# First two tiles of the up product as eight plain block products, with the operand sums of the other units issued behind them

## The chip, the cores and the metric

One NeuronCore of one Trainium2 chip. The time is device microseconds (us) of one launch, which runs a whole encoder layer for two request groups together: 1024 prompt frames and 64 sample frames, 1088 columns in all. The kernel before takes 1810.93 us (median of three executions, 1809.39 to 1812.55).

## The reference, cut to what matters

All arithmetic is float32. The mixers and the memory attention come first, and the change lies where the memory attention ends and the MLP begins:

```
x = x + mix @ w_out
x = x + mem_attend(rmsnorm(x) * norm_mem) @ w_mo
h = rmsnorm(x) * norm_ffn                    # per frame 1/sqrt(mean(x*x) + eps)
x = x + square(relu(h @ w_up)) @ w_down      # w_up 1024 x 4096, w_down 4096 x 1024
y = rmsnorm(x) * norm_final
```

## The kernel before, in words

**Layout.** Activations are held transposed: feature blocks of 128 rows (`KD` = 8 blocks for 1024 features) by frames. The frames are cut into two groups, `GR`: group 0 has 512 columns, group 1 has 576. A float32 product is made of three passes: each operand is cut by `split` (L169 to L171) into a high part (ACT copies it to a rounded type) and a low part (DVE subtracts the high part from the source), and TensorE multiplies high by high, high by low and low by high. So every operand costs one ACT pass and one DVE pass, and every block product three matmuls for each 128-row block.

**The product ahead of the change.** `dense_add(1, w_mo, ...)` adds the memory attention's output to the residual of group 1, in two halves of the contraction. The second half (HALF, `store=True`) goes through the eight output blocks in the order 0, 4, 1, 5, 2, 6, 3, 7. For each block m it loads a 512-column weight tile, splits it, runs 24 matmuls (two column chunks, 320 and 256), adds both chunks to `xT[1][m]` on DVE (L1083), stores the block to HBM (L1085), and then calls `after(m)`, which is `forms`.

**The up product.** h @ w_up is computed in 16 units (`NU`), each giving two 128-row tiles of the hidden layer for both groups. A unit is a 2 x 2 block product (the two halves of the contraction, the two output tiles, the two groups) and is done with seven block products in place of eight: one each with B11, B21, T1, T2, B22, T3 and T4. B11 and B21 are group 0's normalised blocks (`h3`, ready long before). B22 is group 1's blocks 4 to 7. T1 to T4 are sums and differences of blocks of both groups. On the weight side `sums` (four DVE passes) and five `split`s make S1 to S4 and A22 for every unit. Products with group 1 have two column halves of 288, in two PSUM banks (`mul2`); products of group 0 have 512 columns in one bank (`mul`). The `i < 2` branch is another grouping of the same seven products. The squared hidden tiles go to HBM (`hid_d`), to be read again by the down product.

**What `forms` does.** For every m: the square of x (ACT) and its running sum (DVE, L1038), which later becomes the mean square of group 1. From m = 4 on, with k = m - 4: the two blocks k and k + 4 of group 1 are normalised (L1059, with the norm of the layer before, `rm1`), four differences are made (L1270 to L1278) and five operands split (T1, B22, T2, T3, T4). The missing factor between the two norms, `q`, is made from the running sum by a matmul with ones (`pr`) and `rstd_chain` (L149 to L154), and multiplies the unit's results of group 1 in `square`.

**The order of work.** Each engine runs its instructions in the order that a planner wrote. The planner goes through them in its own simulated time, and where several are ready for one engine it takes the one with the lowest `tc.cur_priority`, a number that counts up by one with every instruction issued in the program. The lines that set it here: `dense_add` adds 600 around `after(m)` and takes it off again, and `tc.cur_priority += 1200` (L1284) stands between the dense product and the loop over units. DMAs are issued by SP, in its own queue.

**Buffers.** Raw weights `wr` and split weights `wh`, `wl` have two buffers each. Operands sit in units of 576 columns: `ap` (16), `xt` (16), `aq` (12), `tm` (4), and `fz` (12). The PSUM pool of the loop, `psm`, has two banks `pw` (tag w) and three pairs `pz` (tag z).

Of the kernel before, what the change touches and what calls it, by code (L numbers as in the profile page):

```python
# [9 lines left out]
F32R = mybir.dt.float32r  # L10
# [3 lines left out]
ALU = mybir.AluOpType  # L14
# [3 lines left out]
P = 128  # L18
D = 1024
KD = D // P  # L20
# [32 lines left out]
def kernel(ctx: ExitStack, tc: tile.TileContext, *args):  # L53
    nc = tc.nc
# [10 lines left out]
    w_up, w_down = w_up[0], w_down[0]  # L65
# [103 lines left out]
    def split(hi, lo, src):  # L169
        act(hi, src, AF.Copy)  # L170
        V.tensor_tensor(out=lo, in0=src, in1=hi.bitcast(F32), op=ALU.subtract)  # L171
# [10 lines left out]
    def load_w(src, r0, kt, c0, dst=None):  # L182
        raw = early.pop(c0) if src is w_in and c0 in early else fetch_w(src, r0, kt, c0)
        hi, lo = dst or (wp.tile([P, KD, P], F32R, name=nm, tag=nm) for nm in ("wh", "wl"))
        split(hi[:, :kt], lo[:, :kt], raw)
        return hi, lo
# [35 lines left out]
    def pair(which):  # L222
        return [pools[which].tile([P, 576], F32R, name="ap", tag="ap") for _ in range(2)]
# [18 lines left out]
    with ExitStack() as pa:  # L242
# [5 lines left out]
        xt = []  # L248
# [217 lines left out]
    def halves(t):  # L466
        return t[:, :PAST], t[:, PAST:]
# [551 lines left out]
    def unit(tag, dt=F32):  # L1019
        return units[tag].tile([P, 576], dt, name=tag, tag=tag)  # L1020
# [20 lines left out]
    def rms_stats(g, psum, tag, tiles=None, keep=False, s2=None):  # L1041

        if not s2:
            for k in range(KD):
                s2 = add_square(g, k, s2, wide())
        rr = unit("tm")
        for c0, cn in GR[g][2]:
            ps = psum.tile([P, 512], F32, name="pr", tag=tag)
            mm(ps[:, :cn], ones, s2[:, c0:c0 + cn], True, True)
            v, t = tiles or (unit("tm"), unit("tm"))  # L1050
            rstd_chain(None, cn, ps[:, :cn], "xxx", scale=1.0 / D, out=rr[:, c0:c0 + cn], tiles=(v, t))
            if keep:
                V.tensor_tensor(out=t[:, :cn], in0=v[:, :cn], in1=rr[:, c0:c0 + cn], op=ALU.mult)
                nc.sync.dma_start(out=rms_d[:, c0:c0 + cn], in_=t[:, :cn])
        return rr

    def normed(g, k, gains, rr, c0, cn, out=None):
        hf = unit("tm") if out is None else out
        V.scalar_tensor_tensor(out=hf[:, :cn], in0=xT[g][k][:, c0:c0 + cn], scalar=gains[:, k:k + 1],  # L1059
                               in1=rr[:, c0:c0 + cn], op0=ALU.mult, op1=ALU.mult)  # L1060
        return hf
# [10 lines left out]
    def dense_add(g, src, r0, kt, a, psum, ahead=None, store=False, after=None, order=None):  # L1072

        t0, n, _ = GR[g]
        for m in (0, 4, 1, 5, 2, 6, 3, 7) if after else range(KD):
            w = load_w(src, r0, kt, m * P)
            if ahead:
                ahead(m)
            for c0, cn in GR[g][2]:
                ps = psum.tile([P, 512], F32, name="pa", tag="mm")  # L1080
                mm3(ps[:, :cn], w, lambda k: (a[k][0][:, c0:c0 + cn], a[k][1][:, c0:c0 + cn]), kt, order=order)
                xs = xT[g][m][:, c0:c0 + cn]
                V.tensor_tensor(out=xs, in0=xs, in1=ps[:, :cn], op=ALU.add)  # L1083
            if store:
                nc.sync.dma_start(out=x2_d[m][:, t0:t0 + n], in_=xT[g][m])  # L1085
            if after:
                tc.cur_priority += 600
                after(m)
                tc.cur_priority -= 600
# [135 lines left out]
    def bank():  # L1225
        return psm.tile([P, 512], F32, name="pw", tag="w", bufs=2)

    def banks():
        return psm.tile([P, 2, 512], F32, name="pz", tag="z", bufs=3)
# [4 lines left out]
    def mul(ps, w, b, start, cols):  # L1234

        for k, (bh, bl) in enumerate(b):
            last = k == len(b) - 1
            mm(ps, w[0][:, k], bh[:, cols], start and k == 0, False, skip_group_check=not start)
            mm(ps, w[0][:, k], bl[:, cols], False, False, skip_group_check=not start)
            mm(ps, w[1][:, k], bh[:, cols], False, last, skip_group_check=not start)  # L1240
# [9 lines left out]
    hb = {B11: h3[:4], B21: h3[4:]}  # L1250
    for f in (T2, T1, B22):
        hb[f] = [[late.pop(0)() for _ in range(2)] for k in range(4)]
    for f in (T3, T4):
        hb[f] = [[unit("xt" if k else "ap", F32R) for _ in range(2)] for k in range(4)]

    sums2 = []

    def forms(m):

        if m == 0:  # L1260
            sums2.append(add_square(1, 0, None, unit("tm")))
        else:
            add_square(1, m, sums2[0], unit("tm"))
        if m < 4:
            return
        k = m - 4
        (h11, h12), (h21, h22) = ((xw[0][i], xw[1][i]) for i in (k, k + 4))
        for i in (k, k + 4):
            normed(1, i, g_ffn, rm1, 0, N2, xw[1][i])
        V.tensor_tensor(out=h11[:, :N1], in0=h12[:, :N1], in1=h11[:, :N1], op=ALU.subtract)  # L1270
        act(h11[:, N1:], h12[:, N1:], AF.Copy)
        split(*hb[T1][k], h11)
        V.tensor_tensor(out=h12, in0=h22, in1=h12, op=ALU.subtract)
        split(*hb[B22][k], h22)
        V.tensor_tensor(out=h22, in0=h22, in1=h11, op=ALU.subtract)
        split(*hb[T2][k], h22)
        split(*hb[T3][k], h12)
        V.tensor_tensor(out=h21[:, :N1], in0=h21[:, :N1], in1=h22[:, :N1], op=ALU.subtract)  # L1278
        split(hb[T4][k][0][:, :N1], hb[T4][k][1][:, :N1], h21[:, :N1])

    dense_add(1, w_mo, HALF * P, KD - HALF, om[HALF:], ps1, store=True, after=forms)
    pm1.close()
    psm = ctx.enter_context(tc.tile_pool(name="psm", bufs=2, space=PSUM))
    tc.cur_priority += 1200  # L1284
    for t in t1s:
        Q.memset(t[:, N1:], 0.0)

# [20 lines left out]
    def plus(out, a, b, eng=V):  # L1308
        eng.tensor_tensor(out=out, in0=a, in1=b, op=ALU.add)  # L1309

    for i in range(NU):
        r1 = fetch_w(w_up, 0, KD, 2 * i * P)
        r2 = fetch_w(w_up, 0, KD, (2 * i + 1) * P)
        pa, pb = ([wp.tile([P, KD, P], F32R, name=nm, tag=nm) for nm in ("wh", "wl")] for _ in range(2))
        split(*pa, r1)
        s1 = fz.tile([P, 4, P], F32, name="s1", tag="s1", bufs=1)
        sums(r1[:, :4], r1[:, 4:], r2[:, :4], r2[:, 4:], s1, V)
        S2, S1 = wform(r1[:, :4]), wform(s1)
        S3 = wform(r2[:, :4])
        S4, A22 = [t[:, :4] for t in pb], [t[:, 4:] for t in pb]  # L1320
        split(*S4, r1[:, 4:])
        split(*A22, r2[:, 4:])
        t1 = t1s[i % 2]
        W, Z, X = bank(), banks(), banks()
        mul(W, [t[:, :4] for t in pa], hb[B11], True, slice(0, N1))
        act(t1[:, :N1], W, AF.Copy)
        c12, c22 = unit("ap"), unit("ap")
        if i < 2:

            mul(W, [t[:, 4:] for t in pa], hb[B21], False, slice(0, N1))  # L1330
            Y = banks()
            mul2(Y, S4, hb[B22], True)
            plus(halves(c12), halves(t1), Y[:, :, :HN])
        mul2(Z, S2, hb[T2], True)
        plus(halves(c12), halves(c12 if i < 2 else t1), Z[:, :, :HN])
        mul2(X, S1, hb[T1], True)
        plus(halves(c22), halves(t1), X[:, :, :HN])
        if i < 2:
            plus(halves(c12), halves(c12), X[:, :, :HN])
        else:  # L1340
            mul(W, [t[:, 4:] for t in pa], hb[B21], False, slice(0, N1))
        c11 = unit("xt")
        square(c11[:, :N1], W)
        if i == 0:
            q = rms_stats(1, psm, "w", s2=sums2[0])
            rms = unit("tm")
            nc.sync.dma_start(out=rms, in_=rms_d)
            V.tensor_tensor(out=q, in0=q, in1=rms, op=ALU.mult)
        mul2(Z, S3, hb[T3], False)
        plus(halves(c22), halves(c22), Z[:, :, :HN])  # L1350
        square(c22, c22, q)
        if i >= 2:
            mul2(X, S4, hb[B22], False)
            plus(halves(c12), halves(c12), X[:, :, :HN])
        square(c12, c12, q)
        mul2(Z, A22, hb[T4], False, N1)
        c21 = unit("xt")
        plus(c21[:, :HN], t1[:, :HN], Z[:, 0, :HN])
        plus(c21[:, HN:N1], t1[:, HN:N1], Z[:, 1, :N1 - HN])
        square(c21[:, :N1], c21[:, :N1])  # L1360
        for m, g, t in ((0, 0, c11), (0, 1, c12), (1, 0, c21), (1, 1, c22)):
            t0, n, _ = GR[g]
            nc.sync.dma_start(out=hid_d[2 * i + m][:, t0:t0 + n], in_=t[:, :n])
    fz_ctx.close()


# [122 lines left out]
```

## Time and profile before

| what | value |
|---|---|
| median of three executions | 1810.93 us (1809.39 to 1812.55) |
| the profiled execution: time | 1812.65 us |
| the profiled execution: span, first to last instruction | 1810.6 us |
| mean granted TensorE clock | 0.982 of full |
| PE busy | 1731.0 us, 96% |
| PE weight loads busy | 1516.8 us, 84% |
| DVE busy | 1199.6 us, 66% |
| ACT busy | 794.2 us, 44% |

The span is the profiled execution; its time has 2.05 us more around it. PE is the row of matmuls, DVE the vector engine, ACT the scalar engine. The second half of the dense product ends at 1049.7 us of the span, and the loop over units runs from there to about 1420 us.

### The profile page before, as it was taken

How to read it: one execution, taken by the hardware profiler on the slowest of the kernel's cores; microseconds unless marked ns; L12 is line 12 of the kernel's file. 1: busy time of each engine (PE TensorE's matmuls, PEld its weight loads, DVE VectorE, ACT ScalarE, POOL GpSimd, SP SyncE). 2: the span in 40 equal slices, each digit the busy share in tenths (PEclk: the TensorE clock that was granted, in tenths of full speed). 3: DMA queues.
4: the chain of work that ended last, by engine and by line, in shares of the span. 5: the costliest groups of instructions: out<-in, count | busy, mean ns of one | idle time of the engine just before them, and what ended most of it. 6: DMA issues, size and time to landing. Idle time of an engine off the chain costs nothing.

```text
span 1810.6 us, 29643 instructions
## 1 busy us (share of the span) xinstructions
PE 1731.0 (96%) x11454; PEld 1516.8 (84%) x11467; DVE 1199.6 (66%) x2362; ACT 794.2 (44%) x1619; POOL 96.9 (5%) x201
## 2 busy tenths in 40 slices
PE   7999999999999998899999959999999999999997
PEld 5877757778877877898899949999999999999987
DVE  6455778979887887856777696555555544444435
ACT  6464566455537843535556443434334312222113
POOL 3011202000220200000000000000000000000000
PEclk9999999999999999999999979999999999999999
DMA  7221212231223456422432322333334833222112
GB/s 243 83 77 37 64 46 75 69 82 60 84 89 98 139 159 214 119 85 63 142 104 72 95 85 95 98 104 104 116 105 133 317 97 97 96 90 66 47 35 100
DMA packets 227596, 184.87 MB, mean 102 GB/s; under 512 B 16510, under 2 KB 196415, under 8 KB 227455
## 3 DMA queue, kind: packets, MB, share of 16 engines
q1 hardware_dynamic: 227199, 182.96, 32.5%
q8 instruction: 90, 1.47, 0.4%
q14 instruction: 51, 0.42, 0.1%
q0 software_dynamic: 256, 0.01, 0.1%
HBM read 132.45 MB, written 50.44 MB: 101 GB/s over the span
## 4 chain that ended last, share of the span: by engine, by line
PE 56%; DVE 4%; ACT 1%; DMA 1%; issue 1%; DVEq 0%; ACTq 0%
PE pz L71 24%; PE pw L71 16%; PE pa L71 8%; PE pq L71 5%; PE pmo L71 1%; PE pms L71 1%; DVE y L767 0%; PE pmt L1144 0%; DVE ap L171 0%; PE pz L1414 0%; DVE wl L171 0%; ACT wh L74 0%; DVE tm L1059 0%; DVE xt L1083 0%; DVE xt L1059 0%
## 5 line engine op out<-in xcount | busy, mean ns | idle before, releaser
L74 ACT ACTIVATE wh<-wr 128x1024 fp32r<-128x1024 f32 (+1 forms) x180 | 161.4, 905 | 426.4 <-PE pz L71 195.4
L171 DVE TENSOR_TENSOR wl<-wr,wh 128x1024 fp32r<-128x1024 f32 (+1 forms) x180 | 184.8, 1034 | 67.9 <-ACT wh L74 66.9
L71 PE MATMUL pw<-ap,wh 128*128 128x512 f32 x704 | 220.0, 394 | 1.3 <-ACT t L74 0.7
L71 PE MATMUL pa<-ap,wh 128*128 128x512 f32 (+2 forms) x768 | 192.1, 337 | 5.4 <-DVE xt L1083 3.3
L71 PE MATMUL pz<-ap,wh 128*128 128x288 f32 x960 | 192.5, 294 | 0.0
L71 PE MATMUL pm<-hx,wh 128*128 128x512 f32 (+1 forms) x640 | 178.4, 366 | 2.0 <-ACT wh L74 2.0
L71 PE MATMUL pm<-ap,wh 128*128 128x256 f32 (+1 forms) x768 | 164.9, 308 | 0.0
L71 PEld LDWEIGHTS pz<-ap,wh 128*128 128x128 f32 x960 | 156.7, 188 | 4.9 <-DVE ap L1309 0.4
L71 PEld LDWEIGHTS pa<-ap,wh 128*128 128x128 f32 x768 | 134.6, 194 | 17.7 <-DVE xt L1083 3.4
L71 PEld LDWEIGHTS pw<-ap,wh 128*128 128x128 f32 x704 | 127.8, 189 | 23.8 <-ACT t L74 1.2
L71 PE MATMUL pw<-ap,wl 128*128 128x512 f32 x352 | 138.2, 392 | 5.6 <-DVE wl L171 5.6
L71 PE MATMUL pz<-ap,wl 128*128 128x288 f32 x480 | 141.0, 294 | 0.0
L71 PE MATMUL pa<-ap,wl 128*128 128x512 f32 (+2 forms) x384 | 128.8, 337 | 2.8 <-DVE wl L171 2.8
L71 PEld LDWEIGHTS pm<-hx,wh 128*128 128x128 f32 x640 | 111.3, 192 | 21.8 <-ACT wh L74 2.6
L71 PEld LDWEIGHTS pm<-ap,wh 128*128 128x128 f32 x768 | 124.1, 192 | 5.2 <-issue 1.9
L767 DVE SCALAR_TENSOR_TENSOR y<-ext,cwT,y 128x288 f32<-128x288 f32 (+2 forms) x300 | 125.3, 443 | 3.1
L1309 DVE TENSOR_TENSOR xt<-xt,pz 128x576 f32<-128x576 f32 x56 | 42.2, 753 | 114.4 <-PE pz L71 107.9
L71 PE MATMUL pm<-ap,wl 128*128 128x256 f32 (+1 forms) x384 | 114.3, 298 | 0.0
L71 PE MATMUL pm<-hx,wl 128*128 128x512 f32 (+1 forms) x320 | 112.8, 353 | 0.2 <-DVE wl L171 0.2
L1309 DVE TENSOR_TENSOR xt<-xt,pw 128x512 f32<-128x512 f32 (+2 forms) x80 | 51.0, 638 | 70.0 <-PE pw L71 67.7
L71 PE MATMUL pq<-ap,wh 128*128 128x512 f32 (+2 forms) x384 | 93.1, 331 | 0.0
L74 ACT ACTIVATE sba<-sba 128x127 f32<-128x127 f32 (+8 forms) x102 | 68.1, 682 | 55.2 <-DVE sba L490 54.4
(371 smaller groups left out, 3647.4 us busy)
## 6 DMA issues: line engine op xcount, KB each, us to landing
wr<-in_w_up_dram SPq DMA_DIRECT2D x32, 512.0 KB
wr<-in_w_down_dram SPq DMA_DIRECT2D x32, 512.0 KB
wr<-in_w_in_dram SPq DMA_DIRECT2D x24, 512.0 KB
hid_d<-ap SPq DMA_DIRECT2D x32, 288.0 KB
aq<-hid_d SPq DMA_DIRECT2D x32, 288.0 KB
wr<-in_w_out_dram SPq DMA_DIRECT2D x16, 512.0 KB
wr<-in_w_mq_dram SPq DMA_DIRECT2D x16, 512.0 KB
wr<-in_w_mo_dram SPq DMA_DIRECT2D x32, 256.0 KB
```

Source lines behind the costliest of these rows:

```text
L71: nc.tensor.matmul(out, lhsT=lhsT, rhs=rhs, start=start, stop=stop, **kw)
L74: nc.scalar.activation(out=out, in_=in_, func=func, **kw)
L171: V.tensor_tensor(out=lo, in0=src, in1=hi.bitcast(F32), op=ALU.subtract)
L767: V.scalar_tensor_tensor(out=y[:, :n], in0=ext[:, j:j + n], scalar=cwT[:, ct, j:j + 1], in1=y[:, :n], op0=ALU.mult, op1=ALU.add)
L1309: eng.tensor_tensor(out=out, in0=a, in1=b, op=ALU.add)
```

## The change

- `forms(m)` is cut in two. `second(m)`, called after each dense block as before, makes the square and the running sum, normalises block m of group 1 in place, and splits it: blocks 4 to 7 into B22 as before, blocks 0 to 3 into a new operand `b12`, eight units of the second `ap` pool. `forms(k)` keeps the four differences and the splits of T1, T2, T3, T4, and is called four times inside unit 1, behind the split of that unit's first weight tile.
- Unit 0 becomes a plain product: two weight tiles (`load_w`: no sums, one split each), for each tile a 512-column product over all eight blocks of group 0 (`W`) and a 576-column product over `b12` and B22 (`Z`). `q` is made between the W and the Z products. The results go through `square` alone.
- The loop starts at unit 1, which takes the branch that units 0 and 1 took. T3 and T4 are allocated after the dense product. `tc.cur_priority += 1200` is gone. The stores of a unit are now a function.

```diff
-    def forms(m):
+    b12 = [pair(1) for k in range(4)]
+    def second(m):
         if m == 0:
             sums2.append(add_square(1, 0, None, unit("tm")))
         else:
             add_square(1, m, sums2[0], unit("tm"))
-        if m < 4:
-            return
-        k = m - 4
+        normed(1, m, g_ffn, rm1, 0, N2, xw[1][m])
+        split(*(hb[B22][m - 4] if m >= 4 else b12[m]), xw[1][m])
+
+    def forms(k):
         (h11, h12), (h21, h22) = ((xw[0][i], xw[1][i]) for i in (k, k + 4))
-        for i in (k, k + 4):
-            normed(1, i, g_ffn, rm1, 0, N2, xw[1][i])
...
-        split(*hb[B22][k], h22)
...
-    dense_add(1, w_mo, HALF * P, KD - HALF, om[HALF:], ps1, store=True, after=forms)
+    dense_add(1, w_mo, HALF * P, KD - HALF, om[HALF:], ps1, store=True, after=second)
...
-    tc.cur_priority += 1200
+    for f in (T3, T4):
+        hb[f] = [[unit("xt" if k else "ap", F32R) for _ in range(2)] for k in range(4)]
...
-    for i in range(NU):
+    ws = [load_w(w_up, 0, KD, m * P) for m in range(2)]
+    tiles = [unit("ap") for _ in range(4)]
+    for m in range(2):
+        W = bank()
+        mul(W, ws[m], hb[B11] + hb[B21], True, slice(0, N1))
+        square(tiles[2 * m][:, :N1], W)
+    q, rms = rms_stats(1, psm, "w", s2=sums2[0]), unit("tm")
+    nc.sync.dma_start(out=rms, in_=rms_d)
+    V.tensor_tensor(out=q, in0=q, in1=rms, op=ALU.mult)
+    for m in range(2):
+        Z = banks()
+        mul2(Z, ws[m], b12 + hb[B22], True)
+        square(halves(tiles[2 * m + 1]), Z[:, :, :HN], halves(q))
+    store_hidden(0, tiles)
+
+    for i in range(1, NU):
...
         split(*pa, r1)
+        if i == 1:
+            for k in range(4):
+                forms(k)
...
-        if i < 2:
+        if i == 1:
```

## Rows read from the trace of the kernel before

**Rows 1.** The page, busy time by engine: us, share of the span, instructions.
```profile
PE 1731.0 (96%) x11454; PEld 1516.8 (84%) x11467; DVE 1199.6 (66%) x2362; ACT 794.2 (44%) x1619; POOL 96.9 (5%) x201
```
**Rows 2.** Engines by stretch: busy us (count) of each, granted clock, DMA share, GB/s.
```profile
1030.00:1049.70 19.70, 19.70 (x150) 19.67 (x148) 18.99 (x34) 11.43 (x19) 0.00 (x0) 1.00 0.63 197
1049.70:1068.90 19.20, 2.31 (x6) 0.80 (x4) 19.12 (x30) 9.28 (x16) 0.00 (x0) 0.57 0.05 17
...
1116.10:1420.00 303.90, 303.90 (x2068) 289.11 (x2067) 174.46 (x264) 123.48 (x199) 0.00 (x0) 1.00 0.37 121
```
**Rows 3.** Waits from 1030 to 1100 us: us in total, times, longest.
```profile
PE pr L71 <- DVE tm L1038: 10.7, 1, 10.7
...
PE pw L71 <- DVE wl L171: 5.6, 1, 5.6
...
ACT wh L74 <- DMA wr<-in_w_up_dram: 2.1, 1, 2.1
...
PE pw L71 <- ACT t L74: 0.7, 1, 0.7
```
**Rows 4.** TensorE's timeline about the end of the dense product: start, us, what.
```profile
1050.48 0.70 PE L71 MATMUL pw<-ap,wh 128*128 128x512 f32 x2 [0.61 <-ACT wh L74]
1061.85 1.43 PE L71 MATMUL pr<-tm,ones 128*128 128x320 f32 x2 [10.66 <-DVE tm L1038]
1068.92 0.79 PE L71 MATMUL pw<-ap,wl 128*128 128x512 f32 x1 [5.64 <-DVE wl L171]
```
**Rows 5.** ACT's timeline: the high half of the first up weight tile.
```profile
1046.64 1.06 ACT L74 ACTIVATE wh<-wr 128x1024 fp32r<-128x1024 f32 x1 [2.05 <-PE pa L71]
```
**Rows 6.** DVE's timeline: the first normalisation and two steps of the mean square.
```profile
1030.21 0.82 DVE L1059 SCALAR_TENSOR_TENSOR xt<-xt,g_ffn,tm 128x576 f32<-128x576 f32 x1 [0.45 <-DMA x_d<-xt]
...
1080.71 0.49 DVE L152 TENSOR_TENSOR tm<-tm 128x320 f32<-128x320 f32 x1 [0.53 <-ACT tm L74]
...
1082.47 0.43 DVE L152 TENSOR_TENSOR tm<-tm 128x256 f32<-128x256 f32 x1
```
**Rows 7.** The chain of waits, in order of time: start, us on the chain, what.
```profile
1045.80 0.67 DVE tm L1038
1046.47 0.73 DVE xt L1059
1047.20 0.33 DVE xt L1083
...
1048.93 0.40 DVE xt L1083
1049.32 0.60 DVE xt L1270
...
1055.11 0.67 DVE aq L171
...
1067.73 1.15 DVE wl L171
...
1068.92 4.44 PE pw L71 x10
...
1091.81 1.61 PE pw L71 x7
...
1101.74 11.66 PE pz L71 x88
1113.40 1.16 PE pw L71 x5
1114.56 2.91 PE pz L71 x24
```
**Rows 8.** Short stretches as TensorE resumes: columns as in Rows 2.
```profile
1068.90:1071.00 2.10, 2.08 (x5) 1.70 (x6) 2.10 (x4) 0.87 (x2) 0.00 (x0) 0.50 0.00 0
1071.00:1073.40 2.40, 2.35 (x6) 1.44 (x5) 2.40 (x5) 0.70 (x2) 0.00 (x0) 0.59 0.00 0
1073.40:1076.00 2.60, 1.97 (x9) 1.63 (x10) 2.60 (x6) 1.18 (x3) 0.00 (x0) 1.00 0.00 0
```

More of the change, by code (lines that the diff above doesn't have):

```diff
@@ L1252 @@
         hb[f] = [[late.pop(0)() for _ in range(2)] for k in range(4)]
-    for f in (T3, T4):
-        hb[f] = [[unit("xt" if k else "ap", F32R) for _ in range(2)] for k in range(4)]
+    b12 = [pair(1) for k in range(4)]
     sums2 = []
-    def forms(m):
+    def second(m):
         if m == 0:
@@ L1309, in plus, with store_hidden @@
         eng.tensor_tensor(out=out, in0=a, in1=b, op=ALU.add)
-    for i in range(NU):
+    def store_hidden(i, tiles):
+        for m, g, t in zip((0, 0, 1, 1), (0, 1, 0, 1), tiles):
+            t0, n, _ = GR[g]
+            nc.sync.dma_start(out=hid_d[2 * i + m][:, t0:t0 + n], in_=t[:, :n])
+    ws = [load_w(w_up, 0, KD, m * P) for m in range(2)]
[13 more added lines that the diff above has]
+    for i in range(1, NU):
         r1 = fetch_w(w_up, 0, KD, 2 * i * P)
@@ L1334 @@
         mul2(Z, S2, hb[T2], True)
-        plus(halves(c12), halves(c12 if i < 2 else t1), Z[:, :, :HN])
+        plus(halves(c12), halves(c12 if i == 1 else t1), Z[:, :, :HN])
         mul2(X, S1, hb[T1], True)
         plus(halves(c22), halves(t1), X[:, :, :HN])
-        if i < 2:
+        if i == 1:
             plus(halves(c12), halves(c12), X[:, :, :HN])
@@ L1343 @@
         square(c11[:, :N1], W)
[L1344 to L1348, printed above, removed]
         mul2(Z, S3, hb[T3], False)
@@ L1351 @@
         square(c22, c22, q)
-        if i >= 2:
+        if i > 1:
             mul2(X, S4, hb[B22], False)
@@ L1360 @@
         square(c21[:, :N1], c21[:, :N1])
-        for m, g, t in ((0, 0, c11), (0, 1, c12), (1, 0, c21), (1, 1, c22)):
-            t0, n, _ = GR[g]
-            nc.sync.dma_start(out=hid_d[2 * i + m][:, t0:t0 + n], in_=t[:, :n])
+        store_hidden(i, (c11, c12, c21, c22))
     fz_ctx.close()
```

## Prediction

> **What bounds the kernel now.** Four views, in this order. The page gives TensorE (PE) 96% of the span [rows 1]: a kernel bound by its products, in which only a hole in PE's row is worth something. The table by stretch finds the hole. From 1049.7 to 1068.9 PE is busy 2.31 us while DVE is busy 19.12 of 19.20; DVE was already full, 18.99 of 19.70, beside the dense product; from 1116.1 to 1420 PE has no idle time at all [rows 2]. So what is won at the opening of the up loop is kept to the end, and nothing else needs to move. The waits say what PE stood for there: 10.7 us for a DVE add of the running sum and 5.6 us for a DVE low part of the first up weight tile [rows 3]. That weight's high part was done at 1046.64 + 1.06 = 1047.7 [rows 5], its low part is taken at 1067.73 [rows 7]: twenty microseconds in which DVE preferred `forms`, because the loop's numbers stand 1200 later. The timeline places it: PE runs two W matmuls at 1050.48, the ones product `pr` at 1061.85, and the W product only from 1068.92 [rows 4].
>
> When it resumes, the granted clock is 0.50 and 0.59 of full, and 1.00 from 1073.4 on [rows 8], its levels being 1.2 and 2.4 GHz: ten 512-column matmuls take 4.44 us, where seven take 1.61 at full clock, 0.23 each [rows 7]. That costs 4.44 - 2.30 = 2.1 us.
>
> **TensorE's side of the change.** At full clock a 512-column matmul costs 0.23 us and a 288-column one 11.66 / 88 = 0.1325 [rows 7]. Unit 0 before: 24 x 0.23 + 96 x 0.1325 + 2.9 for T4's 24 [rows 7] = 21.1 us. Unit 0 after: W 48 x 0.23 = 11.0, Z 96 x 0.1325 = 12.7, together 23.8: 2.7 us more work. Unit 1 is another member of the old branch, 21.1. In exchange W needs only group 0's operands and two weight splits, so it can start where the dense product ends, at 1050.48 [rows 4], and run to 1061.5. Its second weight tile takes its buffer from the last dense block: 1049.7 + 1.06 (ACT) + 1.15 (DVE), about 1052, needed at 1056. Hidden.
>
> **DVE's side.** Which work DVE takes first decides, so I count numbers. A dense block issues some 36 instructions, the eight about 285; unit 0 about 180. So `forms` stand at roughly 470 to 520 from the dense product's start, without any addition, while the eight `second`s stand at 630 to 885, with 600 added. The sums that should be made *behind* unit 0 therefore go *ahead* of what unit 0's Z waits for, wherever their inputs are there: forms(0) as soon as blocks 0 and 4 are normalised, and so on. Only the last pair is held up by its own inputs.
>
> Prices [rows 7]: pass of 576 columns 0.67, of 512 columns 0.60, normalisation 0.73, a dense evacuation 0.40 + 0.33, a whole weight tile 1.15. Steps of the mean square 0.49 and 0.43 [rows 6]. From the first normalisation at 1030.21 (it waits for the block's store [rows 6]) DVE has this ahead of the last low part of B22:
> - dense product: 5 weight parts x 0.60 + 6 x 0.40 + 7 x 0.33 = 7.7
> - unit 0's two weight tiles: 2.3
> - `second`: 8 x 0.73 + 7 x 0.67 + 8 x 0.67 = 15.9
> - `forms` 0 to 2, each 5 x 0.67 + 3 x 0.60 = 5.15 without B22: 15.5; the first three passes of forms(3): 1.9
> - two weight sums of unit 1, whose load is long there: 1.2
> - the mean square: 4 x 0.49 + 4 x 0.43 = 3.7
>
> Together 48.2: B22 is complete at 1078.4. Unit 0's old weight sums, S splits and partial sums are gone from this ledger; the four low parts of `b12` are new in it.
>
> **The sum.** W ends at 1061.5. Z goes on with the blocks that have arrived; 28 of its 32 steps (three matmuls, 0.40) need only the first seven blocks, and fit before 1078.4. The last four end at 1080.0. Unit 1's first weights take the buffers that Z then gives free: 1.06 + 1.15 = 2.2, to 1082.2. Unit 1 itself 21.1, and 0.7 for the evacuation between its two W products [rows 3]: 1104.0. The rest of DVE's work (end of forms(3), q, two squarings, unit 1's other sums and splits, some 9 us) lies beside unit 1's two W products, and the `ap` units for S1 to S3, which `b12` holds until Z ends, come free beside them too; cover 6.2 us from 1082.2, so these are nearly late: without that cover 1 to 3 us. For the clock I take the 2.1 us of the row, since PE waits about ten microseconds once more: 1106.1. Bounds: nothing if the slow matmuls fall while DVE is still late, 6.4 if 16 steps run at half clock. SP's read of `rms_d` waits for a `tm` unit, and only unit 0's and 1's stores stand behind it: nothing. ACT is half idle (9.28 of 19.20 [rows 2]): nothing. A late weight load cost ACT 2.1 us [rows 3]; here the `wr` buffers are free from 1053 and needed at 1080: nothing.
>
> Before, the same point (both units done) is 1114.56 + 2.91 less the 1.16 of unit 2's matmuls that ran ahead [rows 7] = 1116.3. The gain is 10.2 us. The profiled execution's 1812.65 (span 1810.6 and 2.05 around it) becomes 1802.4; the median of the runs is 1.72 below that execution, so 1800.7.
>
> **Rivals.**
> 1. *`second` goes first after all* (a unit that `forms` lacks, or a clock of the planner that is not the chip's). For it: DVE's order is laid by simulated readiness; against: the numbers above. B22 is then complete at 1030.2 + 7.7 + 2.3 + 15.9 = 1056.1, Z does not wait and ends at 1074.2, the W products of unit 1 at 1080.4; but DVE must still make T2 and unit 1's S2 and S4, in all 55 us of work, to 1085.4. Then 15.6 of products and about 1 for the clock: 1102, gain 14.3, 1796.6.
> 2. *The wait is shortened, not removed.* Z's second column halves stand behind the first halves' last block in PE's order: 14 steps, 5.6 us, of which the weights' 2.2 is covered, 3.4 net; and the 16 steps after the wait run at half clock, 4.3 beyond what I counted. Gain 2.5, 1808.4: no change. For it: PE's order is fixed; against: nothing ties one half to the other.
> 3. *Slower: the ones product blocks W.* Before, `pr` stood in PE's order behind two W matmuls and held the engine 10.7 us [rows 3, 4]. Its last add stands ahead of 5.7 of the ledger (the mean square, one difference, the last normalisation and low part): 1072.7. If it stands there again, 46 matmuls follow at 1073.5: 10.6, Z 12.7, unit 1 21.8, clock 2.1, to 1120.7: 4.4 later than before, 1815.3. It decides from about 27 W matmuls behind `pr`. Against: the two W tiles hold both banks of the tag that `pr` needs.
> 4. *TensorE's total decides.* The waits return elsewhere and the added products remain: 1810.93 + 2.7 = 1813.6, within what can't be told from no change. Against: [rows 2] show PE idle beside a full DVE in the stretch that is changed. The Trainium skill's page "Perfetto Trace Analysis", section "Identifying the Most-Contended Engine", says to optimise the engine with the highest occupancy first, which speaks against giving TensorE more to do; the same page allows for regimes in which another engine is the contended one, and this case's stretch is such a one.
>
> **How the numbers follow.** Forecast 0.50, its own range 1797 to 1805 (clock 0 to 6.4, order of the last blocks); rivals 0.23, 0.14, 0.08 and 0.05. About 0.2%, 3.6 us, can be told from no change: faster means under 1807.3. That holds for the forecast, rival 1 and a little under half of rival 2: 0.79. Same: the rest of rival 2, and rival 4: 0.13. Slower: rival 3, 0.08. The range 1794.5 to 1808.5 takes in rival 1 with 2 us to spare and rival 2, and leaves out 3 and 4.
>
> **What would show it.** Right: W without idle from about 1050.5 to 1061.5; then PE waits on a DVE low part of `b12` or B22 for 5 to 12 us, with T1 and T2 of the first blocks made on DVE before the last normalisation; a clock of 0.5 for a few microseconds; both units done near 1106; the loop full afterwards. Wrong: `pr` ahead of W in PE's row; a long wait at T2 in place of Z (rival 1); idle time between later units, which would mean that the units of buffers do not suffice.

## The result, and the profile after

The changed kernel takes 1802.04 us (median of five executions, 1799.59 to 1804.52), the kernel before 1810.58 on the same occasion: ratio 0.9947, interval 0.9934 to 0.9960, a gain of 8.5 us where 10.2 were forecast. A second occasion gave 1799.38 against 1810.27, ratio 0.9944 (0.9932 to 0.9957).

The page by engine, as in [rows 1]:

```profile
PE 1730.9 (96%) x11454; PEld 1517.7 (84%) x11467; DVE 1192.9 (66%) x2351; ACT 793.6 (44%) x1618; POOL 97.5 (5%) x201
```

The totals hardly move; TensorE has the same busy time to 0.1 us and the same share. The table by stretch shows the gain (columns as in [rows 2]). In this execution the dense product ended 2.8 us earlier than in that of before, so compare lengths and not clock times.

```profile
1030.00:1047.10 17.10, 17.09 (x130) 16.88 (x128) 16.46 (x29) 8.89 (x15) 0.00 (x0) 1.00 0.64 200
1047.10:1058.80 11.70, 11.11 (x50) 9.26 (x51) 11.70 (x19) 5.65 (x9) 0.00 (x0) 1.00 0.39 116
1058.80:1064.20 5.40, 2.38 (x19) 2.15 (x17) 5.40 (x9) 2.90 (x6) 0.00 (x0) 1.00 0.00 0
1064.20:1067.90 3.70, 0.57 (x3) 0.34 (x3) 3.70 (x7) 3.10 (x6) 0.00 (x0) 0.76 0.01 2
1067.90:1071.00 3.10, 3.10 (x10) 2.60 (x11) 2.29 (x4) 1.46 (x3) 0.00 (x0) 0.50 0.44 169
1071.00:1074.00 3.00, 3.00 (x17) 2.91 (x16) 2.97 (x6) 2.55 (x5) 0.00 (x0) 0.68 0.00 0
...
1103.00:1407.00 304.00, 303.88 (x2072) 289.44 (x2073) 175.03 (x267) 123.37 (x198) 0.00 (x0) 1.00 0.37 122
```

The 19.2 us with 2.31 us of products of [rows 2] are gone: W fills the first 11. What remains is a hole of some six microseconds beside a DVE that is busy throughout, then six microseconds at a granted clock of 0.50 and 0.68 (0.50 is the lower level, 1.2 GHz), as in [rows 8]. From 1103 on PE is full again. The waits of PE, and its timeline at the places of those of [rows 4]:

```profile
PE pz L71 <- DVE ap L171: 3.1, 1, 3.1
PE pz L71 <- ACT ap L74: 3.1, 1, 3.1
PE pw L71 <- ACT t L74: 1.1, 1, 1.1
PE pz L71 <- DVE ap L1308: 0.6, 1, 0.6
```

```profile
1047.69 0.70 PE L71 MATMUL pw<-ap,wh 128*128 128x512 f32 x2 [0.60 <-DVE xt L1083]
...
1058.65 0.42 PE L71 MATMUL pz<-ap,wh 128*128 128x288 f32 x2
...
1064.24 0.53 PE L71 MATMUL pz<-ap,wh 128*128 128x288 f32 x2 [3.06 <-ACT ap L74]
1067.86 0.61 PE L71 MATMUL pz<-ap,wh 128*128 128x288 f32 x1 [3.09 <-DVE ap L171]
...
1069.46 2.12 PE L71 MATMUL pr<-tm,ones 128*128 128x320 f32 x4
...
1081.40 0.63 PE L71 MATMUL pw<-ap,wh 128*128 128x512 f32 x2
```

W begins at 1047.69, Z (`pz`) at 1058.65, unit 1's W at 1081.40. The first two of the waits are the hole: both are for one operand, the last block of `b12`: first its high part from ACT, then its low part from DVE. DVE's timeline shows why it is late. L1059 is a normalisation in `second`, L1269 the first difference in `forms`; the `aq` row is the low part of T2's first block, the `ap` row that of the last block of `b12`, the `fz` row that of the last block of B22 (the difference that overwrites its source follows at once):

```profile
1027.43 0.82 DVE L1059 SCALAR_TENSOR_TENSOR xt<-xt,g_ffn,tm 128x576 f32<-128x576 f32 x1 [0.45 <-DMA x_d<-xt]
...
1029.13 0.68 DVE L1269 TENSOR_TENSOR xt<-xt 128x512 f32<-128x512 f32 x1
...
1040.14 0.75 DVE L171 TENSOR_TENSOR aq<-xt,aq 128x576 fp32r<-128x576 f32 x1
...
1043.00 0.81 DVE L1059 SCALAR_TENSOR_TENSOR xt<-xt,g_ffn,tm 128x576 f32<-128x576 f32 x1
...
1062.52 0.81 DVE L1059 SCALAR_TENSOR_TENSOR xt<-xt,g_ffn,tm 128x576 f32<-128x576 f32 x1
...
1067.06 0.75 DVE L171 TENSOR_TENSOR ap<-xt,ap 128x576 fp32r<-128x576 f32 x1
...
1068.40 0.81 DVE L1059 SCALAR_TENSOR_TENSOR xt<-xt,g_ffn,tm 128x576 f32<-128x576 f32 x1
...
1070.77 0.49 DVE L149 TENSOR_SCALAR tm<-pr 128x320 f32<-128x320 f32 x1 [0.78 <-PE pr L71]
1071.18 0.75 DVE L171 TENSOR_TENSOR fz<-xt,fz 128x576 fp32r<-128x576 f32 x1
```

The first difference comes 1.7 us after the first normalisation, and T2 of block 0 before the third block is normalised. The sums go ahead of what Z needs. Just before the last low part of B22, DVE also waits 0.78 us for the ones product, which PE runs only inside Z.

One more number is used below: the stage, from the start of the last DVE evacuation of the dense product (L1083) to that of the first of the down product (L1308; L1309 before). These rows of a tile's view give both, as the end of one interval of starts and the beginning of the other, first for the kernel before, then for the one after:

```profile
L1083 DVE TENSOR_TENSOR xt<-xt,pa x72: 411/488/689, 681.0 to 1049.9; 128x512 f32<-128x512 f32 x24, 128x320 f32<-128x320 f32 x24, 128x256 f32<-128x256 f32 x24
L1309 DVE TENSOR_TENSOR xt<-xt,pw x80: 402/686/689, 1420.3 to 1798.5; 128x512 f32<-128x512 f32 x64, 128x320 f32<-128x320 f32 x8, 128x256 f32<-128x256 f32 x8
```

```profile
L1083 DVE TENSOR_TENSOR xt<-xt,pa x72: 411/486/689, 680.3 to 1047.1; 128x512 f32<-128x512 f32 x24, 128x320 f32<-128x320 f32 x24, 128x256 f32<-128x256 f32 x24
L1308 DVE TENSOR_TENSOR xt<-xt,pw x80: 402/686/689, 1408.6 to 1787.0; 128x512 f32<-128x512 f32 x64, 128x320 f32<-128x320 f32 x8, 128x256 f32<-128x256 f32 x8
```

370.4 us before, 361.5 after: the stage explains 8.9 of the two profiled executions' 11.9 us. The other three are the earlier start: the first normalisation, with which the kernels begin to differ, already stands 2.8 us earlier (1027.43 against 1030.21 [rows 6]). That is the spread of executions ahead of the change.

### The profile page after: what moved, and what is told of

Its sections match the earlier page's. It is cut to its first block, busy times and chain, and to the rows that moved or that the text cites. A ratio compares the mean times of both kernels' runs of the same rounds, so it can differ in the third digit from the quotient of the medians.

```text
span 1799.1 us, 29632 instructions
## 1 busy us (share of the span) xinstructions
PE 1730.9 (96%) x11454; PEld 1517.7 (84%) x11467; DVE 1192.9 (66%) x2351; ACT 793.6 (44%) x1618; POOL 97.5 (5%) x201
## 4 chain that ended last, share of the span: by engine, by line
PE 56%; DVE 4%; ACT 1%; DMA 1%; issue 1%; DVEq 0%; ACTq 0%
PE pz L71 23%; PE pw L71 15%; PE pa L71 8%; PE pq L71 5%; PE pmo L71 1%; PE pms L71 1%; DVE ap L171 1%; DVE y L767 1%; PE pmt L1144 0%; DVE wl L171 0%; PE pz L1430 0%; ACT wh L74 0%; DVE tm L1059 0%; PE pr L71 0%; DMA wr<-in_w_up_dram 0%
## 5 line engine op out<-in xcount | busy, mean ns | idle before, releaser
L71 PE MATMUL pz<-ap,wh 128*128 128x288 f32 x988 | 198.8, 294 | 6.8 <-DVE ap L171 3.1
L71 PEld LDWEIGHTS pz<-ap,wh 128*128 128x128 f32 x988 | 161.5, 188 | 12.1 <-DVE ap L171 3.3
L71 PE MATMUL pz<-ap,wl 128*128 128x288 f32 x494 | 145.3, 294 | 0.0
L1308 DVE TENSOR_TENSOR xt<-xt,pz 128x576 f32<-128x576 f32 x56 | 42.2, 753 | 115.8 <-PE pz L71 112.5
L1308 DVE TENSOR_TENSOR xt<-xt,pw 128x512 f32<-128x512 f32 (+2 forms) x80 | 51.0, 638 | 70.5 <-PE pw L71 69.7
L71 PEld LDWEIGHTS pz<-ap,wl 128*128 128x128 f32 x494 | 92.9, 188 | 0.0
```

What stands on the lines that cost most here:

```text
L71: nc.tensor.matmul(out, lhsT=lhsT, rhs=rhs, start=start, stop=stop, **kw)
```

## The experiments

| kernel | time, us | ratio to before (interval) | stage, us |
|---|---|---|---|
| before | 1810.58, 1810.27, 1809.68 | | 370.4 |
| the change | 1802.04 | 0.9947 (0.9934 to 0.9960) | 361.5 |
| e0_again, the change once more | 1799.38 | 0.9944 (0.9932 to 0.9957) | 362.4 |
| e1_sums_later | 1793.27 | 0.9893 (0.9875 to 0.9912) | 352.6 |
| e1_repeated | 1793.20 | 0.9909 (0.9895 to 0.9922) | 353.4 |
| e2_before_number | 1810.23 | 0.9998 (0.9986 to 1.0009) | 371.0 |
| e3_number_back | 1798.99 | 0.9941 (0.9927 to 0.9954) | 359.7 |
| e4_sums_in_dense | 1801.66 | 0.9939 (0.9920 to 0.9957) | 362.2 |
| e5_filler | 1804.10 | 0.9963 (0.9950 to 0.9976) | 363.6 |
| e6_filler_in_wait | 1800.46 | 0.9951 (0.9939 to 0.9963) | 360.6 |
| e7_two_plain_units | 1792.98 | 0.9908 (0.9896 to 0.9921) | 353.6 |
| e8_both_tiles | 1800.54 | 0.9946 (0.9933 to 0.9960) | 360.6 |

Two kernels were run twice: the stage differs by 0.9 us in the change and 0.8 in e1, the median by 2.7 and 0.1. The stage is the finer measure, though of one execution each. The change ran on an occasion of its own (before: 1810.58); e1, e2, e4 and e5 on a second (1810.58), e0, e3, e6 and e7 on a third (1810.27), e8 and e1_repeated on a fourth (1809.68). So only the kernels of one occasion stand side by side, and others are compared by their ratios to before and by the stage. e0_again was expected at 1800 to 1804 and is 0.6 below.

**e1_sums_later: is it the order?**

```diff
         if i == 1:
+            tc.cur_priority += 600
             for k in range(4):
                 forms(k)
+            tc.cur_priority -= 600
```

> The changed kernel with 600 added to the numbers of the four forms(k), so that all eight second(m) go ahead of them on DVE. Theory 1 (what is left of the wait comes from the order: the sums go ahead of what Z needs): TensorE no longer waits inside Z, T1 and T2 are ready late but within a few us of need, and the time is 6 to 9 us below the changed kernel's 1802.0: 1793 to 1796. Theory 2 (DVE's total work sets when two units are done, whichever part comes first): the wait moves from Z to T2 and the time stays at 1800 to 1804.

1793.27 us, and 1793.20 when repeated: 17 below before. The change did not run beside it; its two medians are 6 to 9 us higher, its stages 8 to 10, and the intervals of the ratios lie apart. PE's waits from 1040 to 1420 us are down to three short ones:

```profile
PE pw L71 <- DVE xt L1083: 0.6, 1, 0.6
PE pz L71 <- ACT aq L74: 0.6, 1, 0.6
PE pw L71 <- ACT t L74: 0.6, 1, 0.6
```

DVE's timeline has the last of the eight normalisations ahead of the first two differences, where the change has the first difference behind the first normalisation:

```profile
1049.34 0.82 DVE L1059 SCALAR_TENSOR_TENSOR xt<-xt,g_ffn,tm 128x576 f32<-128x576 f32 x1
...
1053.55 1.29 DVE L1269 TENSOR_TENSOR xt<-xt 128x512 f32<-128x512 f32 x2
```

Theory 1 holds. DVE does the same work in both kernels (2351 instructions, 1192.8 and 1192.9 us); only its order differs, and of a wait for the sums 0.6 us is left (`aq` holds T2 and half of T1). With e7 this is the best version found.

> The kernel with the sums set later once more, beside the one above on the same chip: 1789 to 1796, and 4 us or more below it by either theory.

1793.20, and 7.3 us below e8, a variant of the change that ran beside it (last below).

**e2_before_number: do the loop's numbers alone do it?**

```diff
-    tc.cur_priority += 1200
```
(in the kernel before)

> The kernel before with one line taken out, the 1200 added ahead of the loop of units; all else as before. Theory 1 (the gain comes from the plain products, which need few of DVE's results): the two W products start near 1050 us of the span, but Y and T2 wait for the same sums as before, about 1077, and the time is 1807 to 1811. Theory 2 (the loop's numbers alone made the gain): about 1802.

1810.23, no change. W starts at once, and the old unit 0 then stops inside its seven products, as T1 and T2 are not there:

```profile
PE pz L71 <- ACT fz L74: 7.2, 1, 7.2
PE pz L71 <- ACT aq L74: 1.9, 2, 1.5
```

So taking the line out without the plain products is worth nothing: the new products are what give PE something to do. The old unit 0 with DVE's work in yet another order was not run.

**e3_number_back: the plain products with the old line.**

```diff
     for f in (T3, T4):
         hb[f] = [[unit("xt" if k else "ap", F32R) for _ in range(2)] for k in range(4)]
+    tc.cur_priority += 1200
```

> The changed kernel with the 1200 put back ahead of unit 0, so that the eight second(m) (600 added) go ahead of unit 0, its weights and the sums. Theory 1 (what counts is that the second(m) go ahead of the sums; unit 0's weights are two DVE passes): Z finds its operands, W starts a few us late for its weights; 2 to 5 us above the kernel with the sums set later, 1795 to 1798. Theory 2 (taking the 1200 out is part of the gain, as unit 0 must start at once): 1802 or more.

1798.99, 1 us above what theory 1 allowed and 3 below theory 2: neither fits in full. On the same occasion e0, the change without the line, took 1799.38: the times are the same, and only the stage is 1.8 to 2.7 us shorter with the line. Z no longer waits, W loses 1.4 us for its weights, but a new wait stands at Y, the product of S4 with B22 in unit 1:

```profile
PE pz L71 <- ACT wh L74: 3.7, 1, 3.7
PE pw L71 <- DVE wl L171: 1.4, 1, 1.4
```

```profile
1084.00:1096.00 12.00, 10.56 (x59) 10.22 (x60) 7.37 (x12) 2.90 (x5) 0.00 (x0) 0.72 0.38 109
```

Here the sums come behind the eight `second`s, but mostly ahead of unit 1's own weight sums and splits. e1 puts half of them behind those too: DVE's last weight sum for S4 ends at 1069.3 us there and at 1084.3 here. The two waits, and a granted clock of 0.72 over the twelve microseconds about the end of the first, make most of the 6 to 7 us between the two stages.

**e4_sums_in_dense: does it matter where the program issues the sums?**

```diff
         split(*(hb[B22][m - 4] if m >= 4 else b12[m]), xw[1][m])
+        if m >= 4:
+            forms(m - 4)
...
-        if i == 1:
-            for k in range(4):
-                forms(k)
```
(and T3 and T4 are allocated ahead of the dense product again)

> The changed kernel with forms(k) called again inside the dense product, behind second(k + 4), at the added 600, and nothing of it in unit 1. Theory 1 (on DVE the sums go ahead of unit 0's operands anyway, so where the program issues them matters little): within 2.5 us of the changed kernel, 1799.5 to 1804.5. Theory 2 (issuing the sums behind unit 0 is what gains): back to 1807 or more.

1801.66, stage 362.2: the same as the change, again with a wait of PE for `b12`, in two pieces:

```profile
PE pz L71 <- ACT ap L74: 8.8, 2, 7.3
```

As far as the chip goes, the part of the change that moves the sums behind unit 0 does nothing.

**e5_filler and e6_filler_in_wait: what does PE's idle time cost?** Both add 24 matmuls of 512 columns; e5 into a bank of W's, e6 into a free pair.

```diff
+    W = bank()                                # e6: W = banks(), written at W[:, 0]
+    mul(W, ws[0], hb[B11] + hb[B21], True, slice(0, N1))
     q, rms = rms_stats(1, psm, "w", s2=sums2[0]), unit("tm")
```

> The changed kernel with a third W product (24 matmuls of 512 columns, 5.5 us, its result not read) between W and the mean square. Theory 1 (TensorE waits over 6 us inside Z, then runs some us at half clock): the added products lie in the wait and keep the clock up; time 1799.5 to 1802.5, that is none to 2 us saved. Theory 2 (TensorE's total decides): 5.5 us longer than the changed kernel, 1807.5.

1804.10: neither. e5 doesn't test what it was made for: its bank comes free late, with an evacuation on ACT at 1069.85, so that PE's order has the added products behind the wait, their first part at the low clock; the 24 take 7.08 us, where 24 at full clock take 5.5 (chain of waits):

```profile
1070.39 7.08 PE pw L71 x24
```

> The changed kernel with 24 matmuls of 512 columns more (group 0 by the first weight tile, into a free pair of banks, not read), which stand in TensorE's order between W and the first Z, so ahead of the wait. Theory 1 (TensorE waits there and then runs at half clock): the 5.5 us lie in the wait, the clock stays at full, and 0 to 2 us are saved: 1799.5 to 1802. Theory 2 (TensorE's total decides): 1807.5. If the wait hides the work but the clock costs nothing: 1802 to 1803.

1800.46 against e0's 1799.38 on the same occasion, stage 360.6 against 361.5 and 362.4. Here the products stand between W and Z, the wait shrinks to 0.97 us, and the granted clock stays up (PE's timeline, then the stretches):

```profile
1070.51 0.40 PE L71 MATMUL pz<-ap,wh 128*128 128x288 f32 x1 [0.97 <-DVE ap L171]
```

```profile
1050.00:1067.00 17.00, 16.66 (x74) 13.88 (x75) 17.00 (x26) 8.46 (x15) 0.00 (x0) 1.00 0.26 79
1067.00:1070.50 3.50, 2.54 (x20) 2.31 (x18) 3.50 (x7) 2.91 (x6) 0.00 (x0) 1.00 0.01 2
1070.50:1075.00 4.50, 4.49 (x30) 4.28 (x31) 4.43 (x7) 3.15 (x7) 0.00 (x0) 1.00 0.32 120
```

5.5 us of products cost nothing that can be told from the spread, which rules out that TensorE's total decides. Whether the clock gives time back isn't shown: the stage is 0.9 to 1.8 us shorter, where two executions of one kernel differ by 0.9, and the median is 1.1 longer.

**e7_two_plain_units: the price of a plain unit.** Unit 1 is a second copy of the plain unit 0 (its weights `ws` from column 256 on, the same `q`, `b12` and B22), on top of e1; the sums and the branch of unit 1 move to unit 2, with which the loop begins:

```diff
-    for i in range(1, NU):
+    ws = [load_w(w_up, 0, KD, (2 + m) * P) for m in range(2)]
...
+    store_hidden(1, tiles)
+
+    for i in range(2, NU):
```

> The kernel with the sums set later, and unit 1 a plain product too (its own weights, b12 kept on); the sums then stand in unit 2. In that kernel TensorE waits for about 1 us only, so this prices a plain unit by itself. Theory 1 (a plain unit costs 24 more matmuls of 512 columns for 24 fewer of 288 or 224: 23.8 against 21.1 us): 2.7 us more less what is left of the waits, 1794.5 to 1796.5. Theory 2 (a plain unit is free since it also relieves DVE): 1793.

1792.98 and a stage of 353.6, beside e1's 352.6 and 353.4: the time is theory 2's, 1.5 us below theory 1's range. The chain of waits prices the unit directly, W and Z from 1071.14 to 1094.76:

```profile
1071.14 10.90 PE pw L71 x48
1082.04 12.72 PE pz L71 x96
```

23.6 us, against 21.1 for a unit of the loop, read from two evacuations of the changed kernel on ACT's timeline:

```profile
1128.86 0.60 ACT L74 ACTIVATE t<-pw 128x512 f32<-128x512 f32 x1 [0.55 <-PE pw L71]
...
1150.00 0.60 ACT L74 ACTIVATE t<-pw 128x512 f32<-128x512 f32 x1 [0.55 <-PE pw L71]
```

So the 2.5 us are real, and theory 2 is wrong about the unit itself. But e1's last waits, for ACT's `aq` and `t`, 1.2 us, are gone too. That leaves 1.3; the stages show 0.2 to 1.0 of it and the medians none, which is within what executions differ by.

**e8_both_tiles: PE's own order.**

```diff
+    Zs = [banks() for _ in range(2)]
     for m in range(2):
...
-        mul2(Z, ws[m], b12 + hb[B22], True)
...
+        mul2(Zs[m], ws[m], b12[:3], True)
+    for m in range(2):
+        w = [t[:, 3:] for t in ws[m]]
+        mul2(Zs[m], w, b12[3:] + hb[B22], False)
```

> The changed kernel with both tiles' Z products by the first three blocks of b12 ahead of the rest of Z in the program, so that TensorE's order has 12 steps of three matmuls ahead of its wait, where it had 6. Theory 1 (in the changed kernel the second tile's first steps stood behind the wait, though their operands were there): Z ends 2 to 3 us earlier against the end of the dense product (up to 1 more where less runs at half clock); 1796.5 to 1800. Theory 2 (DVE's last low parts of B22 decide when Z ends): no change, 1799.5 to 1802.

Theory 1 is right about Z and wrong about the time. Z ends 31.3 us after the start of W (1048.68 to 1080.02) where the change needs 33.7 (1047.69 to 1081.40). But 1800.54 and a stage of 360.6 (0.9 to 1.8 us shorter) are no clear gain. Unit 1 now starts sooner and waits at the weights of Y. DVE ends their last sum at 1086.40, but ACT takes the high part only at 1087.66, behind the evacuation of W at 1086.65. PE's timeline at the start of W, the wait inside Z, the start of unit 1's W and the wait at Y:

```profile
1048.68 0.70 PE L71 MATMUL pw<-ap,wh 128*128 128x512 f32 x2 [0.61 <-DVE xt L1083]
...
1068.83 0.61 PE L71 MATMUL pz<-ap,wh 128*128 128x288 f32 x1 [3.08 <-DVE ap L171]
...
1080.02 0.62 PE L71 MATMUL pw<-ap,wh 128*128 128x512 f32 x2
...
1088.34 0.53 PE L71 MATMUL pz<-fz,wh 128*128 128x288 f32 x2 [1.72 <-ACT wh L74]
```

## Why the prediction was right, step by step

- **The bound.** Right: the hole beside a full DVE was what could be won, and the loop stays full afterwards.
- **W.** Forecast 11.0 us from the end of the dense product without idle; measured 1047.69 to 1058.65, 10.96. Right.
- **DVE's order and ledger.** Forecast 48.2 us from the first normalisation to the last low part of B22, with the sums ahead; measured 1027.43 to 1071.93 (1071.18 + 0.75), 44.5. The order is right, and e1 and e4 show that it, not the place in the program, makes the wait. The ledger is 3.7 too long: seven of the mean square's eight steps (3.2), two low parts of T1 (1.3) and T3's and T4's of the first block (1.3) that I had ahead came behind, 5.8 in all, and 1.5 of idle time that I had not counted came in. It cost nothing: PE shows no wait for a low part of B22.
- **Z.** Forecast to end 29.5 us after the start of W, 31.6 with the clock's 2.1; measured 33.7. The wait was 6.2 us, where I had some ten, but the term was undersized by 2.1: it was not DVE's last block that set its end. I let 28 of Z's 32 steps run as their blocks arrive; PE's fixed order had six ahead of the wait for `b12`, and the second tile's first six behind it. e8 moves those six and Z ends 2.4 us sooner. By an estimate from the rows, the 33.7 are 20.2 to the end of the wait, some 25 steps at 0.40 (10.1), the ones product, which I had left out of Z (1.1 at full clock, by e7's chain of waits), and 2.3 for the clock.
- **The 2.2 us for unit 1's weights.** Did not come: the chain goes from Z to unit 1's W without a wait, as the first tile's Z ended well before the second's and gave its buffer back: ACT took the new weights' high part at 1077.21, DVE had the low part by 1079.5. Oversized by 2.2, so this error cancels that of Z, and that is luck.
- **Unit 1.** Forecast 21.8 with the evacuation; measured 1081.40 to 1104.9 (1106.29 less 1.38 for the time of six W matmuls of unit 2 that ran ahead), 23.5. "Nearly late" is where it went: 1.1 for the evacuation of W where 0.7 was forecast, 0.6 for a DVE sum, the rest in smaller pieces. With it the sum is 57.2 us from the start of W to the end of both units, where 55.6 were forecast and 65.8 measured before; a gain of 8.6, 1.6 below the forecast. The end is read from the chain of waits:

```profile
1103.12 3.17 PE pz L71 x24
1106.29 1.38 PE pw L71 x6
```

- **Rival 1** was not this kernel but is e1. Its price, 1796.6, was 3.3 too high: I held all products of unit 1 but W until the last part of T2; in e1 they begin as parts arrive.
- **Rivals 2 to 4.** The ones product stood behind W, inside Z (1069.46), so W was not blocked. Z's halves did not queue one behind the other, the tiles did. TensorE's total is ruled out by e6.

Left open: whether e6's clock gives any time back, and what spreads the stretches ahead of the change.

## What to carry to other kernels

When an engine off the main path has a backlog, a product that costs TensorE more but needs less of that engine can be worth its price: here 2.5 us of products more, for a stage shorter by 8 to 9. What it buys is the length of the wait, less the products, and no more than the backlog lets through behind it. Then look at the numbers by which work is ordered, not at the place where it stands in the program: work issued later can still go first. The best further step was an offset that puts each piece of DVE's work in the order in which TensorE needs it.

## What the runs showed of the hardware that was not expected

The twelve profiled executions run the same products up to the dense product's end, but that end (the last L1083) lies anywhere from 1044.3 us (e1) to 1051.6 us (e4). The first L1083, before any of the changes, already starts anywhere from 676.7 us (e7) to 682.1 us (e4). A difference of a few microseconds between two profiled spans therefore says little of a change that acts later; the length of the stage does.
